# Column sums of the second norm in two groups, their last squares added on VectorE, and two chains of weight sums woven together

## The chip, the cores and the metric

The kernel runs on one core of one Trainium2 chip. The metric is the device time of one execution in microseconds; lower is better. Inputs and outputs are float32 and lie in device memory (HBM).

## The reference

One decoder layer on 1024 tokens with 1024 channels, and a final norm. Cut to what matters here:

```python
xn = rmsnorm(x, norm_mix_w)
proj = xn @ w_in                              # 1024 x 4352: queries, keys, values, gates
merged = sigmoid(g_da) * (diff_attention(...) @ w_br_da) + sigmoid(g_sw) * (window_attention(...) @ w_br_sw)
x = x + merged @ w_mix_out
xn = rmsnorm(x, norm_ffn_w)                   # x * rsqrt(mean(x*x) + eps) * w, per token
u = xn @ w_up                                 # 1024 x 5632
c = causal depthwise convolution of width 3 over u, + bias
gate, val = split(c)
x = x + (silu(gate) * val) @ w_down
return rmsnorm(x, norm_final_w)
```

## The kernel before

**Layout.** All activations are held transposed: 128 channels on the partitions, the 1024 tokens along the free dimension, cut into two halves of 512. Each float32 operand is split into a rounded high part (a cast on ScalarE, names that end in `h`) and a low part (the difference, on VectorE, names that end in `l`); one product of 128 x 128 weights with 512 tokens is then three matmuls: high by high, high by low, low by high.

**Products.** The large products (projections, mix, up projection, down projection) take a pair of weight chunks at once by a Strassen-Winograd scheme: seven products P1 to P7 of twelve matmuls each (4 chunks of the contraction by 3) instead of eight. Their operands are the blocks and some sums of them: `A11`, `A12`, `A22`, `S1` to `S4` of the weights, `B11`, `B21`, `B22`, `T1` to `T4` of the activations. Each product fills one PSUM bank (tiles `t`, 8 banks in rotation), so the eighth bank after it must be free again. `recombine` (L502 to L521 hold its callers and steps) empties them: one copy on ScalarE (`s`, L512) and seven steps on VectorE (L514 to L521), which give the two output chunks `us`.

**Stages.** `project` does the projections: five plain chunks, then nine pairs (`self.pairs`). `attention` follows, with some gate products between. `rest` merges the branches; `mix` does the mixing product and builds the operands of the up projection; `hidden` runs the up projection over 22 pairs `j` (a gate chunk and a value chunk each), with convolution and gating behind each pair; `down` does the down projection and the last norm.

**Order.** Each engine runs its instructions in one fixed order; a scheduler makes it from the order in the program, and the program bends it. `issue_after(i)` says that what is traced in its block stands behind `i` on that engine; it is an order, not a wait. In `mix` the work is laid out by a table `due`, whose entries are two letters: for instance `h40 l40` are the high and low part of T4's block 0. Each entry joins the end of one of two chains, `tails[0]` on VectorE and `tails[1]` on ScalarE.

**The second norm.** It needs, per token, the sum of squares over all channels. ScalarE squares each chunk of x; GpSimd adds the squares into `acc` (the tile `rstd`, one row of 512 for each half of the tokens, L945). The last four squares of the first half of the tokens (`self.sq`, in two tiles named `rv`) are not added to it. `col_sums` (L207) then sums over the partitions with matmuls of one column against a vector of ones: for each block of 128 tokens one matmul for each tile that is to be summed, so 4 x 5 for the first half and 4 x 1 for the second. `rstd_cols` makes the mean (`ms`, VectorE, L214) and its power -1/2 (GpSimd, L216); `spread` (L222) lays the result along the tokens, and ScalarE copies it into `rstd` (L1158). In the up projection the norm is applied late, to the products: L1235 multiplies `us` with `rstd`, ahead of the convolution (L1249, L1251, L1252).

In `hidden`, pair 0 runs P1, P5, P3, P7, P6, then the column sums, then P2 and P4. P4 needs T4, whose splits are the last entries of `due`.

**Weight sums.** The Strassen sums S1 to S4 of the projections' weights are made on GpSimd (L143 to L146, tiles `sf`) from two loaded chunks (`raw`, `rv`). For the mix weights (`md`) and the first two pairs of the up weights (`ud`, NPRE = 2) they are made by DMA in device memory, during the projections: copies issued by SyncE (L97, L109) and adding DMAs issued by GpSimd (L98, L110). `sums_of` (for md) is 32 such steps and `sums_up` (for ud) 16; a step that adds goes onto what a copy step before it wrote. The loop over the nine pairs takes a few steps of the chained generators in each pair: six in pairs 0 to 5, four in pairs 6 to 8; first all steps of md, then those of ud. SyncE's steps stand behind the pair's weight load, GpSimd's behind the pair's four sums.

For pair 1 of the up projection the weights come ready from `ud`: `part_pair` loads, casts and splits them in four parts, A11 and A12, S1 and S2, S3 and S4, A22 (L121, L126, L128). From pair 2 on `sum_pair` and `split_pair` do it (L138 to L146, L157, L159). The buffers of `raw` are three, so a load waits until the third part before it is split.

Of the kernel before, what the change touches and what calls it, by code (L numbers as in the profile page):

```python
# [3 lines left out]

# [1 line left out]

# [12 lines left out]
P = 128  # L19
# [4 lines left out]
H2 = 512  # L24
# [4 lines left out]
NPRE = 2  # L29
# [17 lines left out]
class Trunk:  # L47
# [27 lines left out]
    def ahead(self, n):  # L75
        while len(self.wq) < n and self.wsrc and (self.wsrc[0][1] != "pair" or self.uw):
            src, nk, *eng = self.wsrc.pop(0)
            if nk == "pair":
                first, skip = eng or (False, 0)
                if len(src) == 3:  # L80
                    w = {}
                    for part in range(4):
                        w.update(self.part_pair(src, part))
                    self.wq.append(w)
                else:
                    self.wq.append(self.split_pair(*self.sum_pair(src, first), skip))
            else:
                self.wq.append(self.load_w(src, nk, *eng))
        for i in range(min(2, len(self.wsrc)) if self.deep else 0):
            if len(self.wsrc[i]) == 2:  # L90
                self.wsrc[i] += None, None, self.load_raw(*self.wsrc[i])

    def sums_of(self, d, src, n):

        nc = self.nc
        row = lambda m, r: src[m].rearrange("p k c -> p (k c)")[:, r * n:(r + 1) * n]
        copy = lambda n, src: lambda m: nc.sync.dma_start(d[n][m], src(m))  # L97
        add = lambda n, o, r: lambda m: nc.gpsimd.dma_start(d[n][m], row(m + o, r), accum_op=ALU.add)  # L98
        for step in (copy("P5", lambda m: row(m + 4, 0)), copy("P7", lambda m: row(m + 4, 0)), add("P5", 4, 1), add("P7", 0, 0),
                     copy("P6", lambda m: d["P5"][m]), add("P6", 0, 0), copy("P3", lambda m: d["P6"][m]), add("P3", 0, 1)):  # L100
            for m in range(4):
                step(m)
                yield

    def sums_up(self):

# [201 lines left out]
    def project(self):  # L308
# [6 lines left out]
        with ExitStack() as ctx:  # L315
# [7 lines left out]
            acc = self.rstd  # L323
# [3 lines left out]
            ps = [[bank() for _ in range(2)] for _ in range(3)]  # L327
# [44 lines left out]
            with tc.tile_pool(name="xrp", bufs=6, reuse_waits="tile") as xrp:  # L372
# [69 lines left out]
                ssq = bank()  # L442
# [31 lines left out]
            for m in self.plain[3:]:  # L474
# [4 lines left out]
                if m == self.plain[3]:  # L479
                    with tc.issue_after(self.pow.ins), tc.high_priority(40):  # L480
                        wg, pg = self.next_w(), [bank() for _ in range(2)]
                    for hf in range(2):
                        self.mm3(pg[hf], wg, self.xact, hf)
            prods = (("P1", "A11", "B11"), ("P2", "A12", "B21"), ("P5", "S1", "T1"), ("P7", "S3", "T3"), ("P3", "S4", "B22"),
                     ("P6", "S2", "T2"), ("P4", "A22", "T4"))
            sums = chain(self.sums_of(self.md, self.w_mix, H2), self.sums_up())
            for j, ms in enumerate(self.pairs):
                w = self.next_w()
                for _ in range(6 if j < 6 else 4):
                    with tc.issue_after(self.sync), tc.issue_after(self.sum):  # L490
                        next(sums, None)
                pp = {}
# [400 lines left out]
    def mix(self, M, mr, mctx):  # L893
# [82 lines left out]
        def run_due(i, m):  # L976
            for op in due.pop((i, m), "").split():
                ops[op[:-1]](int(op[-1]))
# [81 lines left out]
                    sqs[:] = [self.tl(uw, [P, 2, H2], "rv", bufs=2) for _ in range(2)]  # L1060
        self.uw = uw
        run_due(13, 1)
        assert not due
        self.tails = tails
        return w0

    def chain(self, tails, n, f, *a):

        with self.tc.issue_after(tails[n]):
            i = f(*a)  # L1070
        tails[n] = i.ins
        return i
# [12 lines left out]
    def hidden(self, w0):  # L1085
        nc, tc = self.nc, self.tc
        with self.hctx as ctx:
# [7 lines left out]
            for j in range(NF):  # L1095
                w, ps = ready.pop(j) if j else (w0, {})
                if j == 0:
# [6 lines left out]
                        ps[name] = self.tl(psF, [P, H2], "t")  # L1104
                        self.product(ps[name], w[a], b)
                    ssq = self.tl(psF, [P, H2], "t")
                    self.col_sums(ssq, [self.rstd[:, :H2], *self.sq], 4, 0)
                    self.col_sums(ssq, [self.rstd[:, H2:]], 4, 4)
                    with tc.high_priority(400), tc.issue_after(self.tails[0]):
                        rs = self.rstd_cols(ssq, 8, D)  # L1110
                    self.tails[0] = self.ms
                if j == NF - 1:
                    for n in range(2):
                        self.wsrc[n] += None, None, self.load_raw(*self.wsrc[n])
# [377 lines left out]
```

## Time and profile before

| | us |
|---|---|
| median of 3 runs | 1324.23 (1322.56 to 1325.07) |
| profiled execution, its own time | 1323.9 |
| its span on the core | 1321.8 |
| busy in the span: TensorE matmuls / weight loads | 1307.1 / 1089.1 |
| busy: VectorE / ScalarE / GpSimd | 1067.7 / 639.5 / 497.5 |

The span is the time from the first to the last instruction. The engines are named PE (TensorE matmuls), PEld (its weight loads), DVE (VectorE), ACT (ScalarE), POOL (GpSimd) and SP (SyncE); a q behind a name is its sequencer, which issues DMAs. A row of the timeline has the start and the duration in us, the engine, the line, the operation, out<-in by the program's names, the shape and the count of instructions merged in it; in brackets the idle time ahead of it and what ended it. Matmuls are pipelined: a matmul of 512 columns is shown with a duration of 0.39 us, though the next one starts 0.23 us later, so the pace is read from start to start. A group row has the busy time in us and the mean duration of one instruction in ns. A row of the list of waits has who waited for whom, the total in us, how often, and the longest.

### The profile page before, as it was taken

The page shows a single profiled execution, that of the slowest core. Times are in us where ns is not written, and L with a number is a line of the kernel's source. Part 1 is how long each engine was busy: PE and PEld are TensorE (multiplying, and loading weights), DVE is VectorE, ACT ScalarE, POOL GpSimd, SP SyncE. Part 2 cuts the span into 40 slices and gives each one's busy share as a digit, 9 for nine tenths or more (in the row PEclk, how much of TensorE's full clock was granted, in tenths as well). Part 3 has the DMA queues.
Part 4 walks back from the last instruction along what each step waited for, and adds up shares of the span by engine and source line. Part 5 has one row for each costly group of instructions (what it writes and reads, how often), then busy time and mean ns, then how long its engine had stood idle before and what let it go on. Part 6 is the DMA issues. An engine that isn't in the chain of part 4 may idle for free.

```text
span 1321.8 us, 17377 instructions
## 1 busy us (share of the span) xinstructions
PE 1307.1 (99%) x6194; PEld 1089.1 (82%) x6194; DVE 1067.7 (81%) x1512; ACT 639.5 (48%) x1010; POOL 497.5 (38%) x399
## 2 busy tenths in 40 slices
PE   9999999999999999999999999999999999999997
PEld 7888888788888878888888888888888888888886
DVE  8845764488888977657889999999999999896865
ACT  8522331276666765334764344344344335554543
POOL 0456675001111015753335566766766632000002
PEclk9999999999999999999989999999999999999999
DMA  8357977976544335659665436554626228953534
GB/s 301 127 151 209 256 184 197 304 202 169 139 131 117 124 120 207 168 169 291 187 177 175 152 123 165 140 202 134 210 86 163 88 76 268 334 173 117 165 98 147
DMA packets 85447, 229.58 MB, mean 174 GB/s; under 512 B 9457, under 2 KB 17265, under 8 KB 85105
## 3 DMA queue, kind: packets, MB, share of 16 engines
q1 hardware_dynamic: 63264, 187.04, 42.7%
q0 software_dynamic: 9216, 24.12, 10.9%
q10 hardware_dynamic: 12880, 17.31, 3.7%
q8 instruction: 49, 0.80, 0.3%
q14 instruction: 38, 0.30, 0.1%
HBM read 173.39 MB, written 84.41 MB: 195 GB/s over the span
## 4 chain that ended last, share of the span: by engine, by line
PE 85%; POOL 4%; issue 3%; DVE 3%; DMA 3%; ACT 2%; SPq 0%; POOLq 0%; DVEq 0%; ACTq 0%
PE t L1082 34%; PE y L1305 9%; PE d L1305 7%; PE m L1046 6%; PE g L199 4%; PE g L200 4%; PE g L201 4%; PE sc L687 3%; POOL us L502 2%; PE t L703 1%; PE t L207 1%; DMA ud<-in_w_up 1%; PE sc L200 1%; PE sc L199 1%; PE sc L201 1%
## 5 line engine op out<-in xcount | busy, mean ns | idle before, releaser
L180 DVE TENSOR_TENSOR wl<-raw,wh 128x1024 fp32r<-128x1024 f32 (+2 forms) x91 | 109.2, 1201 | 48.5 <-ACT wh L178 40.5
L178 ACT CAST wh<-raw 128x1024 fp32r<-128x1024 f32 (+2 forms) x91 | 80.5, 886 | 99.7 <-PE y L1305 49.6
L1235 POOL TENSOR_TENSOR us<-us,rstd 128x1024 f32<-128x1024 f32 x42 | 93.4, 2272 | 51.0 <-DVE us L520 31.2
L216 POOL TENSOR_TENSOR rs<-ms,mhalf 128x8 f32<-128x8 f32 (+2 forms) x9 | 13.3, 1477 | 237.2 <-DVE ms L214 231.0
L143 POOL TENSOR_TENSOR sf<-rv 128x512 f32<-128x512 f32 x29 | 56.1, 1936 | 109.1 <-DMA rv<-in_w_up 53.9
L159 DVE TENSOR_TENSOR sl<-sf,sh 128x1024 fp32r<-128x1024 f32 x58 | 76.4, 1317 | 9.8 <-ACT sh L157 9.8
L157 ACT CAST sh<-sf 128x1024 fp32r<-128x1024 f32 x58 | 60.2, 1046 | 45.0 <-POOL us L1234 21.8
L1249 ACT ACTIVATE c<-us,vecs 128x1024 f32<-128x1024 f32 x44 | 54.7, 1247 | 52.9 <-POOL us L1235 49.8
L1082 PE MATMUL t<-x,wh 128*128 128x512 f32 x240 | 79.7, 389 | 0.0
L199 PE MATMUL g<-xh,wh 128*128 128x512 f32 x176 | 71.1, 404 | 2.5 <-ACT g L616 1.4
L1252 DVE SCALAR_TENSOR_TENSOR c<-us,vecs,c 128x1024 f32<-128x1024 f32 x44 | 73.3, 1698 | 0.0
L1082 PE MATMUL t<-x,sh 128*128 128x512 f32 x220 | 72.6, 398 | 0.0
L200 PE MATMUL g<-x,wh 128*128 128x512 f32 x176 | 70.5, 401 | 0.0
L201 PE MATMUL g<-xh,wl 128*128 128x512 f32 x176 | 70.4, 400 | 0.0
L1251 DVE SCALAR_TENSOR_TENSOR c<-us,vecs,c 128x1024 f32<-128x1024 f32 x44 | 65.1, 1512 | 1.7 <-ACT c L1249 1.7
L145 POOL TENSOR_TENSOR sf<-raw,rv 128x512 f32<-128x512 f32 x29 | 54.1, 1866 | 32.1 <-DVE sl L159 32.1
L1305 PE MATMUL y<-h,wh 128*128 128x512 f32 (+1 forms) x224 | 65.3, 375 | 0.0
L159 DVE TENSOR_TENSOR wl<-raw,wh 128x1024 fp32r<-128x1024 f32 x29 | 63.1, 2175 | 0.3
L691 DVE CUSTOM_DVE_ANT_0 L<-sc,bias 128x128 f32<-128x128 f32 (+7 forms) x64 | 47.7, 752 | 17.9 <-PE sc L687 14.7
L670 POOL MEMSET aT<- 128x128 f32 x32 | 6.2, 205 | 142.2 <-PE t L716 103.9
L692 ACT ACTIVATE L<-L,sm 128x128 f32<-128x128 f32 (+7 forms) x64 | 49.6, 778 | 20.6 <-DVE sm L691 17.9
L1046 PE MATMUL m<-x,wh 128*128 128x512 f32 x192 | 58.9, 389 | 0.0
(349 smaller groups left out, 4094.7 us busy)
## 6 DMA issues: line engine op xcount, KB each, us to landing
u<-qd SPq DMA_DIRECT2D x72, 256.0 KB, 6.4
raw<-in_w_in SPq DMA_DIRECT2D x22, 512.0 KB, 5.6
raw<-in_w_up SPq DMA_DIRECT2D x22, 512.0 KB, 5.0
hd<-c SPq DMA_DIRECT2D x22, 512.0 KB, 2.6
sdP<-in_w_down POOLq DMA_DIRECT2D x16, 704.0 KB, 8.3
rv<-in_w_up SPq DMA_DIRECT2D x20, 512.0 KB, 4.2
hc<-hd SPq DMA_DIRECT2D x33, 256.0 KB, 5.2
gr<-gd SPq DMA_DIRECT2D x16, 512.0 KB, 4.6
```

The lines of the kernel that those rows point to most:

```text
L159: low = nc.vector.tensor_tensor(lo, src, hi.bitcast(F32), ALU.subtract)
L178: self.hi = nc.scalar.copy(wh, raw)
L180: self.lo = (eng or nc.vector).tensor_tensor(wl, raw, wh.bitcast(F32), ALU.subtract)
L199: nc.tensor.matmul(ps, wh[:, kc + o, :], ah, start=first and n == 0, stop=False)
L200: nc.tensor.matmul(ps, wh[:, kc + o, :], al, start=False, stop=False)
L201: nc.tensor.matmul(ps, wl[:, kc + o, :], ah, start=False, stop=last and n == len(kcs) - 1)
L1046: nc.tensor.matmul(ps, v[:, m % 2 * 4 + k, :], x, start=start and k == j == 0, stop=k == 3 and j == 2, skip_group_check=True)
L1082: nc.tensor.matmul(ps, (ah, ah, al)[p][:, k, :], (bh, bl, bh)[p], start=first and n == p == 0, stop=last and p == 2 and n == len(ks) - 1, ...
L1235: i = (nc.vector if m % NF == 0 else nc.gpsimd).tensor_tensor(us[:, 2:], us[:, 2:], self.rstd, ALU.mult)
L1251: nc.vector.scalar_tensor_tensor(c, us[:, 1:T + 1], cw[1], c, ALU.mult, ALU.add)
L1252: nc.vector.scalar_tensor_tensor(c, us[:, 0:T], cw[0], c, ALU.mult, ALU.add)
L1305: nc.tensor.matmul(ps, v[:, k - k0, :], x, start=start and k == i == 0, stop=k == HK - 1 and i == 2, skip_group_check=True)
```

## The change

The last four squares of the first half are added into `acc` by VectorE, at the end of `mix`, behind the splits of T4. The column sums then read `acc` alone, 4 + 4 matmuls instead of 20 + 4, and stand in two groups: those of the second half at the old place, those of the first half behind P2 and P4. In `ahead`, parts 1 to 3 of pair 1's weights stand behind `ms` on VectorE and part 0 no longer does (before, all four did, since `self.tails[0]` was set to `ms`). In the projections the steps of the two chains are woven: in turn four of md and two of ud, six in each of the first eight pairs and none in the ninth.

```diff
@@ ahead
                     for part in range(4):
-                        w.update(self.part_pair(src, part))
+                        with self.tc.issue_after(self.ms) if part else nullcontext():
+                            w.update(self.part_pair(src, part))
@@ new
+    def weave(self, *gens):
+
+        for _ in range(8):
+            for g, n in zip(gens, (4, NPRE)):
+                for _ in range(n):
+                    next(g)
+                    yield
@@ project
-            sums = chain(self.sums_of(self.md, self.w_mix, H2), self.sums_up())
+            sums = self.weave(self.sums_of(self.md, self.w_mix, H2), self.sums_up())
             for j, ms in enumerate(self.pairs):
                 w = self.next_w()
-                for _ in range(6 if j < 6 else 4):
+                for _ in range(6):
                     with tc.issue_after(self.sync), tc.issue_after(self.sum):
                         next(sums, None)
@@ mix
         run_due(13, 1)
+        for sq in self.sq:
+            add(acc[:, :H2], sq)
@@ hidden
                     ssq = self.tl(psF, [P, H2], "t")
-                    self.col_sums(ssq, [self.rstd[:, :H2], *self.sq], 4, 0)
                     self.col_sums(ssq, [self.rstd[:, H2:]], 4, 4)
+                    for i in (1, 6):
+                        name, a, b = prods[i]
+                        ps[name] = self.tl(psF, [P, H2], "t")
+                        self.product(ps[name], w[a], b)
+                    self.col_sums(ssq, [self.rstd[:, :H2]], 4, 0)
                     with tc.high_priority(400), tc.issue_after(self.tails[0]):
                         rs = self.rstd_cols(ssq, 8, D)
-                    self.tails[0] = self.ms
```

Line numbers shift by 8 to 13 behind the new function: the changed kernel's L215 is `col_sums` (L207 before), L222 is `ms` (L214), L1080 the chained work of `mix` (L1070), L1092 the products (L1082), L510 the product of `us` with `rstd` (L502), L118 the adding DMA into ud (L110).

TensorE at the start of the up projection, before. `t_6546` is the bank of P6, `t_6559` that of the column sums, `t_6588` that of P2, `t_6601` that of P4; of the rows of the column sums those of one block of tokens and of the second half are shown:

```order
L1082 MATMUL t_6546<-z_1093_6231,sl_6197 128x512
L207 MATMUL t_6559<-ones,rstd 128x1
L207 MATMUL t_6559<-ones,rv_6334 128x1 x2
L207 MATMUL t_6559<-ones,rv_6333 128x1 x2
...
L207 MATMUL t_6559<-ones,rstd 128x1 x4
L1082 MATMUL t_6588<-x_1110_6399,sh_6152 128x512 x2
...
L1082 MATMUL t_6601<-T_3_6332,wl_6474 128x512
```

And in the changed kernel, with `t_6550` the bank of P6, `t_6563` that of the column sums, `t_6568` that of P2, `t_6581` that of P4 and `t_6666` that of P1 of pair 1:

```order
L1092 MATMUL t_6550<-z_1093_6231,sl_6197 128x512
L215 MATMUL t_6563<-ones,rstd 128x1 x4
L1092 MATMUL t_6568<-x_1110_6399,sh_6152 128x512 x2
...
L1092 MATMUL t_6581<-T_0_6329,wh_6472 128x512 x2
...
L1092 MATMUL t_6581<-T_3_6332,wl_6474 128x512
L215 MATMUL t_6563<-ones,rstd 128x1 x4
L1092 MATMUL t_6666<-B_0_5751,wh_6618 128x512 x2
```

The sixteen matmuls that read the squares are gone, and four of the eight left stand behind P4.

VectorE from the last split of T4, before. `u` and `us` are the recombination of pair 0, `ms` the mean, `wl_6632`, `sl_6638`, `sl_6644`, `wl_6650` the low parts of pair 1's weights, `sl_6668` and `wl_6664` the first ones of pair 2's:

```order
L1070 TENSOR_TENSOR T_3_6332<-xm_5769,T_3_6332 128x512
L515 TENSOR_TENSOR u_1132_6617<-t_6546,s_1131_6616 128x512
L214 TENSOR_SCALAR ms_6584<-t_6559 128x8
L516 TENSOR_TENSOR u_1133_6618<-u_1132_6617,t_6533 128x512
L128 TENSOR_TENSOR wl_6632<-raw_6628,wh_6630 128x1024
L128 TENSOR_TENSOR sl_6638<-raw_6634,sh_6636 128x1024
L514 TENSOR_TENSOR us_6614<-s_1131_6616,t_6588 128x512
...
L159 TENSOR_TENSOR sl_6668<-sf_6656,sh_6666 128x1024
L514 TENSOR_TENSOR us_6796<-s_1172_6798,t_6691 128x512
L159 TENSOR_TENSOR wl_6664<-raw_6652,wh_6662 128x1024
L1235 TENSOR_TENSOR us_6614<-us_6614,rstd 128x1024
```

And in the changed kernel (`wl_6620`, `sl_6626`, `sl_6632`, `wl_6638` for pair 1, `wl_6652` and `sl_6656` for pair 2):

```order
L1080 TENSOR_TENSOR rstd<-rstd,rv_6334 128x512 x2
L1080 TENSOR_TENSOR rstd<-rstd,rv_6333 128x512 x2
L136 TENSOR_TENSOR wl_6620<-raw_6616,wh_6618 128x1024
L523 TENSOR_TENSOR u_1132_6605<-t_6550,s_1131_6604 128x512
...
L529 TENSOR_TENSOR us_6603<-u_1133_6606,t_6581 128x512
L222 TENSOR_SCALAR ms_6598<-t_6563 128x8
L136 TENSOR_TENSOR sl_6626<-raw_6622,sh_6624 128x1024
...
L167 TENSOR_TENSOR wl_6652<-raw_6640,wh_6650 128x1024
L167 TENSOR_TENSOR sl_6656<-sf_6644,sh_6654 128x1024
L1248 TENSOR_TENSOR us_6602<-us_6602,rstd 128x1024
```

The four adds are new; all seven steps of pair 0's recombination (L522 to L529) now stand ahead of `ms`, and parts 1 to 3 of pair 1's weights behind it.

GpSimd from the sums of the last pair of the projections, before (`ud_92` and `ud_93` are the two pairs of the up weights, `us` the projections' outputs):

```order
L145 TENSOR_TENSOR sf_1670<-raw_1665,rv_1667 128x512
L146 TENSOR_TENSOR sf_1670<-raw_1665,sf_1669 128x512
L110 DMA ud_92<-in_w_up 128x512
L502 TENSOR_TENSOR us_1644<-us_1644,rstd 128x1024
L110 DMA ud_93<-in_w_up 128x512
L110 DMA ud_92<-in_w_up 128x512
L110 DMA ud_93<-in_w_up 128x512
L502 TENSOR_TENSOR us_1786<-us_1786,rstd 128x1024
```

And in the changed kernel, where `mdP_90` is the last of the mix sums:

```order
L153 TENSOR_TENSOR sf_1672<-raw_1667,rv_1669 128x512
L154 TENSOR_TENSOR sf_1672<-raw_1667,sf_1671 128x512
L98 DMA mdP_90<-in_w_mix 128x512
L510 TENSOR_TENSOR us_1646<-us_1646,rstd 128x1024
L98 DMA mdP_90<-in_w_mix 128x512 x3
L118 DMA ud_92<-in_w_up 128x512
L118 DMA ud_93<-in_w_up 128x512
L510 TENSOR_TENSOR us_1790<-us_1790,rstd 128x1024
```

The last adds into `ud` were four, of two kinds, in the last two pairs; they are now two, behind those of the mix sums. Further up, pairs 2, 3, 5 and 7 have four adds into `md` and two into `ud` each, and pairs 0, 1, 4 and 6 none; before, pairs 1, 2 and 3 had four adds, 6 had four, and 4, 5, 7 and 8 two each.

1 line of the change is left out of this document (removed).

## The prediction

> **What bounds the kernel now.** I read the page first, then the stages (the table of windows), then the rows of each engine in order of time around the places that the change touches, then the list of waits. Page, part 1, and two kinds of windows (time busy on PE, PEld, DVE, ACT, POOL, then granted clock, DMA share, GB/s):
>
> ```profile
> PE 1307.1 (99%) x6194; PEld 1089.1 (82%) x6194; DVE 1067.7 (81%) x1512; ACT 639.5 (48%) x1010; POOL 497.5 (38%) x399
> 682.45:685.10 2.65, 2.65 (x26) 2.61 (x24) 2.65 (x6) 2.65 (x5) 0.00 (x0) 1.00 0.09 29
> 685.10:690.22 5.12, 5.12 (x26) 5.12 (x25) 1.61 (x3) 2.13 (x3) 0.10 (x1) 0.50 0.45 135
> 690.22:695.35 5.13, 5.13 (x13) 4.07 (x14) 3.03 (x4) 0.00 (x0) 3.99 (x4) 0.50 0.67 224
> 704.00:1099.00 395.00, 395.00 (x1748) 327.15 (x1747) 385.50 (x337) 163.10 (x173) 244.72 (x173) 1.00 0.46 140
> ```
>
> TensorE is busy nearly always, so time can come only from work that it need not do, from work that it does slowly, or from its few stalls. The windows show slow work: from 685.10 to 695.35, 10.25 us, its clock was granted at 0.50. And in the hidden stage (704 to 1099) VectorE is busy 385.50 of 395.00 us: TensorE is the bound, but VectorE stands 2.4% behind it.
>
> TensorE's rows there, with the first column sum, the last eight passes, the first matmuls of P2 and P4 of pair 0, P1 of pair 1, the spread of rstd and P5 of pair 1; ahead of them the column sums of the first norm, at 39 us:
>
> ```profile
> 39.36 1.84 PE L207 MATMUL t<-ones,rstd 128*128 128x1 f32 x16
> 41.07 0.48 PE L199 MATMUL t<-xh,wh 128*128 128x512 f32 x1
> 682.54 0.28 PE L207 MATMUL t<-ones,rstd 128*128 128x1 f32 x2
> 688.58 1.84 PE L207 MATMUL t<-ones,rstd 128*128 128x1 f32 x8
> 690.29 1.20 PE L1082 MATMUL t<-x,sh 128*128 128x512 f32 x2
> 695.47 0.62 PE L1082 MATMUL t<-T,wh 128*128 128x512 f32 x2
> 698.22 0.61 PE L1082 MATMUL t<-B,wh 128*128 128x512 f32 x2
> 703.66 1.03 PE L222 MATMUL t<-ident,rs 128*128 128x128 f32 x8
> ```
>
> A column sum is two passes, so the 24 of them are 48 passes. At full clock sixteen passes took 41.07 - 39.36 = 1.71 us (0.107 each) and the clock did not fall. The 48 ran from 682.54 to 690.29, 7.75 us, and the clock fell 2.6 us into them. P2's twelve matmuls behind them took 5.18 us (690.29 to 695.47), P4's twelve 2.75 (695.47 to 698.22).
>
> **Column sums: TensorE's side.** Before, 682.54 to 695.47 is 12.93 us for 48 passes and P2. The change leaves 16 passes, eight and eight with P2 and P4 between, and drops 32. Neither group (0.86 us) is as long as the 1.71 us that kept the clock at 1.00, so I take full clock: 1.71 + 2.75 = 4.46 us. Saved: 8.47 us.
>
> Not all arrives, since the second group waits for four adds on VectorE, and the spread for the norm. VectorE, GpSimd, SyncE and ScalarE there:
>
> ```profile
> 683.62 2.48 DVE L1070 TENSOR_TENSOR T<-xm,T 128x512 fp32r<-128x512 f32 x4
> 690.47 0.17 DVE L214 TENSOR_SCALAR ms<-t 128x8 f32<-128x8 f32 x1 [3.76 <-PE t L207]
> 692.28 1.22 DVE L128 TENSOR_TENSOR sl<-raw,sh 128x1024 fp32r<-128x1024 f32 x1
> 695.67 0.69 DVE L514 TENSOR_TENSOR us<-s,t 128x512 f32<-128x512 f32 x1 [2.17 <-PE t L1082]
> 697.47 2.25 DVE L128 TENSOR_TENSOR sl<-raw,sh 128x1024 fp32r<-128x1024 f32 x1
> 701.44 2.31 DVE L159 TENSOR_TENSOR sl<-sf,sh 128x1024 fp32r<-128x1024 f32 x1
> 704.71 1.53 DVE L159 TENSOR_TENSOR wl<-raw,wh 128x1024 fp32r<-128x1024 f32 x1
> 706.17 3.45 DVE L1235 TENSOR_TENSOR us<-us,rstd 128x1024 f32<-128x1024 f32 x2
> 690.72 1.66 POOL L216 TENSOR_TENSOR rs<-ms,mhalf 128x8 f32<-128x8 f32 x1 [4.45 <-DVE ms L214]
> 697.34 1.30 POOL L144 TENSOR_TENSOR sf<-sf,raw 128x512 f32<-128x512 f32 x1 [2.64 <-DMA raw<-in_w_up]
> 693.52 0.33 SPq L138 DMA_DIRECT2D raw<-in_w_up  x1
> 703.63 1.05 ACT L157 CAST wh<-raw 128x1024 fp32r<-128x1024 f32 x1 [1.86 <-PE t L1082]
> ```
>
> T4's splits end at 686.10 in either kernel. An add of 512 columns is costed like one of them, 0.60: the four end at 688.5. TensorE reaches the second group at 682.54 + 0.86 + 2 x 2.75 = 688.9, so the adds are just hidden; if they were not, each 0.1 us late is 0.1 us on TensorE. Then VectorE, in its new order: the low part of pair 1's first weights (1.14 from start to next start), seven steps of the recombination (0.60 each) and only then ms: 688.5 + 1.1 + 4.2 = 693.8, ms by 694.0, the power by 695.7. TensorE has done P1 and P2 of pair 1 by 688.9 + 0.86 + 5.5 = 695.3 and waits 0.4 us for the spread. It starts that at 695.7 and no longer at 703.66: TensorE gains 8.0 us there.
>
> **Column sums: VectorE's side.** The change gives VectorE 2.4 us of adds and lets it drop its waits of 3.76 us (for the column sums) and 2.17 us (for P2). New is a wait further on: SyncE's load of pair 2's raw weights follows the first split of pair 1's sums, which begins at 692.28 before and at 694.0 now. So it goes out at about 695.2, not 693.52, and lands 3.8 us later as before (693.52 to 697.34), at 699.0; with ScalarE's cast of 1.05 us, the two splits of L159 (1.53 and 2.31) end at about 703.9, and the product with rstd (L1235) starts there and not at 706.17. VectorE gains 2.3 us where TensorE gains 8.0: it is 5.7 us further behind from there on. Moving parts 1 to 3 of pair 1's weights behind ms costs nothing by itself: their first reader, P5 of pair 1, stands behind the spread.
>
> What can TensorE bear? The bank that P6 of a pair needs is freed by L518; the matmul with a low part waits for L180:
>
> ```profile
> 1065.40 0.68 DVE L518 TENSOR_TENSOR u<-u,t 128x512 f32<-128x512 f32 x1
> 1069.04 0.61 PE L1082 MATMUL t<-z,sh 128*128 128x512 f32 x2
> 1103.89 0.96 DVE L180 TENSOR_TENSOR wl<-raw,wh 128x768 fp32r<-128x768 f32 x1 [1.50 <-ACT wh L178]
> 1127.49 0.95 DVE L180 TENSOR_TENSOR wl<-raw,wh 128x768 fp32r<-128x768 f32 x1
> 1129.34 0.39 PE L1305 MATMUL d<-x,wl 128*128 128x512 f32 x1
> ```
>
> Late in the hidden stage the bank is free 1069.04 - 1066.08 = 2.96 us ahead, at the start of the down projection the weights 1129.34 - 1128.44 = 0.90 us. TensorE keeps of its 8.0 us what VectorE gained plus this margin: 2.3 + 0.9 = 3.2 by the tighter place, 2.3 + 3.0 = 5.3 by the other. Between the two places VectorE idles 1.50 us in one wait, which a late VectorE can use, but that wait is for a cast that TensorE's own progress releases. I take 3.8, nearer to the tighter place since it comes last.
>
> [...]
>
> **The woven sums.** The number of copies (48) and adds is the same; only their order changes. TensorE's waits in this stage, and their cause:
>
> ```profile
> PE g L199 <- DVE u L518: 1.1, 1, 1.1
> PE t L1082 <- DVE wl L159: 0.6, 1, 0.6
> POOL ud L110 <- DMA ud<-ud: 12.2, 2, 7.7
> 227.02 0.82 POOL L110 DMA_DIRECT2D ud<-in_w_up  x1 [4.46 <-DMA ud<-ud]
> 227.57 2.69 POOL L502 TENSOR_TENSOR us<-us,rstd 128x1024 f32<-128x1024 f32 x1
> 230.29 1.15 ACT L533 ACTIVATE hi<-us,vecs 128x1024 fp32r<-128x1024 f32 x1 [12.60 <-POOL us L502]
> 87.27 2.72 POOL L98 DMA_DIRECT2D mdP<-in_w_mix  x3
> ```
>
> Before, the last adds into ud stand on GpSimd in the same pair as the copy that they add to and wait 12.2 us for it; the product us is queued behind, ScalarE's cast behind that, VectorE's recombination behind that, and the first gate product waits 1.1 us for a bank. Woven, each add follows its copy by a whole pair (19.0 us: 84 matmuls at 395.00/1748), and the last pair has none. In pair 1 the three adds ahead of us (2.72 us) go too, and with them the lateness behind the 0.6 us wait. I count both: 1.7 us. Bounds: 0, and those 1.7 us. SyncE's copies from md and ud likewise wait for adds a pair or more old, so raw loads behind them are not held.
>
> **Sum.** 1.7 + 3.8 = 5.5 us. The profiled execution took 1323.9 us (span 1321.8 and 2.1 around it), 0.3 below the median of the runs, so I set no difference between the two: 1318.4 us.
>
> **Rivals.** (a) TensorE keeps all 8.0: 1323.9 - 1.7 - 8.0 = 1314.2. For it: not one wait of TensorE in the hidden stage. Against: a lag of 5.7 against margins of 3.0 and 0.9.
> (b) VectorE is the bound throughout, no margin is left: 1323.9 - 1.7 - 2.3 = 1319.9. For it: 97.6% busy; against: the 2.96 us.
> (c) VectorE gains nothing, because the raw load or GpSimd's sums come over 2 us later than worked out (SyncE now issues two large copies of the down weights ahead of these loads): only the margin of 0.9 and the 1.7 are left, 1321.3, or 1322.2 without the margin.
> (d) Slower: GpSimd becomes the bound in the projections. Four pairs now issue six adds each where the fullest before issued four. These rows give its work in such a pair:
>
> ```profile
> L98 POOL DMA_DIRECT2D mdP<-in_w_mix x16 | 15.7, 1105 | 0.6 <-issue 0.6
> L502 POOL TENSOR_TENSOR us<-us,rstd 128x1024 f32<-128x1024 f32 x15 | 43.6, 2971 | 2.8 <-DVE us L520 2.8
> 84.32 1.29 POOL L145 TENSOR_TENSOR sf<-raw,rv 128x512 f32<-128x512 f32 x1 [1.16 <-DVE sl L159]
> ```
>
> Six issues of 1.105, two products of 2.971 and four sums of 1.29 make 17.7 us; it decides above the pair's 19.0. If the two issues more (2.2 us) came to lie on TensorE's path in all four pairs, that is 8.8 us, without the 1.7: 1323.9 - 3.8 + 8.8 = 1328.9. Against it: by this sum 1.3 us of each such pair are left, and the extra issues stand behind both products of their pair.
> That the clock still falls I hold unlikely, and it would change little, since VectorE then sets the end all the same.
>
> **How the numbers follow.** What this measurement can tell from no change is about 0.2%, 2.6 us. Chances: forecast 0.50, (a) 0.15, (b) 0.13, (c) 0.13, (d) 0.09. Forecast, (a) and (b) lie below 1321.6, and of (c) a small part: faster 0.80. The rest of (c) and a weak (d): same 0.11; slower 0.09. The forecast's own range is 3.2 to 5.3 us with 0 to 1.7 us: 1316.9 to 1320.7. The range to state reaches to (a) and past (c): 1313.9 to 1323.2.
>
> **What would show it.** Clock 1.00 all through 680 to 700, and P4 of pair 0 directly behind P2; the second eight passes at about 689 with a wait under 0.3 us; spread at about 694 (1.7 earlier than 695.7), some 0.4 us of waiting. VectorE's first product with rstd some 4 us earlier than 706.17. Then, late in the hidden stage and at the start of the down projection, TensorE waits for L518 and for low parts, 4 us in sum; if there are none, it is (a). In the projections no wait for ud on POOL and no gap at the first gate product. The prediction is wrong if waits for VectorE start already at pair 2, if POOL's sums are late in pairs 2 to 7, or if the attention stage, which I leave as it is, shifts by over 1 us.

## The result and the profile after

The change made the kernel slower, not faster: 1328.33 us (median of 7 runs, 1327.06 to 1330.39) against 1322.56 us for the kernel before in the same sessions, a ratio of 1.0044 with a 95% interval of 1.0027 to 1.0061. The profiled execution, the slowest of the seven, took 1330.39 us with a span of 1328.6 us. The forecast was 1318.4.

| from the starts of matmuls, us | before | after |
|---|---|---|
| first gate product (the projections are done) | 237.96 | 244.27 |
| first column sum | 682.54 | 689.03 |
| first matmul of the down projection (`y`) | 1098.96 | 1102.75 |
| first matmul of its second chain (`d`) | 1128.88 | 1134.93 |
| end of the span | 1321.8 | 1328.6 |

So the projections cost 6.3 us, and the place of the column sums and the 400 us behind it, 446.34 before and 445.90 after from the first column sum to `d`, gave back 0.4. That 0.4 is what remains of three parts: up to the spread 6.38 us were saved (14.74 in place of 21.12), then 3.68 lost in the hidden stage (398.98 from the spread to `y`, in place of 395.30) and 2.26 from `y` to `d` (32.18 in place of 29.92). What is left of the difference in span, some 0.7 us, lies behind `d`.

At the column sums, the page's line on TensorE and VectorE and the table of windows (time busy on PE, PEld, DVE, ACT, POOL, then granted clock, DMA share, GB/s), kernel after:

```profile
PE 1304.9 (98%) x6162; PEld 1081.4 (81%) x6162; DVE 1076.9 (81%) x1516; ACT 636.2 (48%) x1010; POOL 502.7 (38%) x399
689.03:692.00 2.97, 2.97 (x19) 2.60 (x18) 2.97 (x6) 2.35 (x4) 0.00 (x0) 1.00 0.21 65
692.00:696.38 4.38, 4.38 (x25) 3.53 (x23) 4.28 (x7) 1.72 (x2) 0.23 (x3) 1.00 0.53 143
696.38:703.77 7.39, 5.73 (x26) 4.40 (x26) 7.32 (x12) 1.11 (x2) 2.63 (x2) 1.00 0.96 332
```

The clock stays at 1.00 here, and TensorE is idle only for the 1.66 us ahead of the spread. Its rows and those of the other engines there, in order of time for each engine, kernel after:

```profile
689.03 0.95 PE L215 MATMUL t<-ones,rstd 128*128 128x1 f32 x8
695.46 1.05 PE L215 MATMUL t<-ones,rstd 128*128 128x1 f32 x8
696.38 0.70 PE L1092 MATMUL t<-B,wh 128*128 128x512 f32 x2
703.77 1.09 PE L230 MATMUL t<-ident,rs 128*128 128x128 f32 x8 [1.66 <-POOL rs L224]
692.56 2.85 DVE L1080 TENSOR_TENSOR rstd<-rstd,rv 128x512 f32<-128x512 f32 x4
700.90 0.16 DVE L222 TENSOR_SCALAR ms<-t 128x8 f32<-128x8 f32 x1
700.98 2.35 DVE L136 TENSOR_TENSOR sl<-raw,sh 128x1024 fp32r<-128x1024 f32 x2
708.89 1.35 DVE L167 TENSOR_TENSOR wl<-raw,wh 128x1024 fp32r<-128x1024 f32 x1 [4.36 <-ACT wh L165]
712.40 4.54 DVE L1248 TENSOR_TENSOR us<-us,rstd 128x1024 f32<-128x1024 f32 x2
716.86 3.51 DVE L1264 SCALAR_TENSOR_TENSOR c<-us,vecs,c 128x1024 f32<-128x1024 f32 x2
733.55 2.42 DVE L167 TENSOR_TENSOR wl<-raw,wh 128x1024 fp32r<-128x1024 f32 x1
696.95 1.17 SPq L97 DMA_DIRECT2D sdP<-in_w_down  x2
702.22 2.07 SPq L146 DMA_DIRECT2D raw<-in_w_up  x3
707.80 1.05 ACT L165 CAST wh<-raw 128x1024 fp32r<-128x1024 f32 x1 [5.67 <-DMA raw<-in_w_up]
707.86 1.30 POOL L152 TENSOR_TENSOR sf<-sf,raw 128x512 f32<-128x512 f32 x1 [2.79 <-DMA raw<-in_w_up]
711.34 2.27 POOL L154 TENSOR_TENSOR sf<-raw,sf 128x512 f32<-128x512 f32 x1
```

From the first column sum to the first matmul of pair 1, TensorE took 7.35 us (689.03 to 696.38) where it took 15.68 before (682.54 to 698.22): 8.33 saved. VectorE shows where they went. To compare times, 6.49 is taken off (689.03 - 682.54). SyncE issues the first raw load of pair 2 at 695.73 (before: 693.52), behind two copies for the down projection's sums; GpSimd can go on with that pair's sums at 701.37 (697.34), ScalarE casts at 701.31, and VectorE, after a wait of 4.36, reaches the first product with rstd at 705.91 (706.17). It has gained 0.26 us, and loses more than that behind it: the product takes 4.54 and the first two steps of the convolution 3.51 where before they took 3.45 and 2.48, and GpSimd's sums run at the same time. In the kernel before, GpSimd was idle there for 6.19 us. The split of pair 3's first weights, at 727.06, is 2.35 us later than before (two rows of the kernel before, GpSimd's and VectorE's):

```profile
713.59 0.10 POOL L1234 MEMSET us<- 128x2 f32 x1 [6.19 <-DVE c L1252]
724.71 3.09 DVE L159 TENSOR_TENSOR wl<-raw,wh 128x1024 fp32r<-128x1024 f32 x1
```

TensorE, still 6.4 us ahead at the spread (697.28 against 703.66), therefore waits. Its list of waits in the kernel after (who for whom, total, times, longest):

```profile
PE t L1092 <- ACT wh L165: 3.8, 1, 3.8
PE t L230 <- POOL rs L224: 1.7, 1, 1.7
PE t L1092 <- DVE wl L167: 1.6, 2, 1.1
PE t L1092 <- DVE u L523: 1.3, 3, 0.6
PE y L1318 <- DVE wl L188: 1.2, 1, 1.2
```

The first and third lie in the projections. The other three are new, and lie at the up and the down projection: the spread, a PSUM bank that VectorE empties late (L523), and a late low part at the start of the down projection (`y`). Behind the spread the list thus names 2.5 us, while the starts of the matmuls show 5.9 lost (3.68 and 2.26); the rest is in delays too small for it. The last wait has a link of its own, again from the kernel after: ahead of that low part VectorE waits for SyncE's load of `x`. SyncE issues it at 1120.61, behind a weight load that goes out at 1118.89, when a split on VectorE ends.

```profile
1129.16 0.69 DVE L1324 TENSOR_TENSOR x<-x,y 128x512 f32<-128x512 f32 x1 [1.25 <-DMA x<-x2d]
1131.83 0.50 PE L1318 MATMUL y<-x,wl 128*128 128x512 f32 x1 [1.19 <-DVE wl L188]
```

The largest wait is in the projections, and it is new. GpSimd, SyncE, ScalarE and TensorE there, kernel after:

```profile
173.84 2.81 POOL L98 DMA_DIRECT2D mdP<-in_w_mix  x3
182.46 0.81 POOL L118 DMA_DIRECT2D ud<-in_w_up  x1 [2.47 <-DVE u L526]
178.89 6.73 SPq L97 DMA_DIRECT2D mdP<-mdP  x3
189.53 2.42 SPq L117 DMA_DIRECT2D ud<-ud  x2
192.68 0.38 SPq L546 DMA_DIRECT2D qd<-hi  x1
189.22 1.15 ACT L541 ACTIVATE hi<-us,vecs 128x1024 fp32r<-128x1024 f32 x1 [10.54 <-POOL us L510]
200.00 1.04 ACT L544 CAST hi<-us 128x1024 fp32r<-128x1024 f32 x1 [8.64 <-DMA qd<-hi]
200.95 1.04 ACT L165 CAST wh<-raw 128x1024 fp32r<-128x1024 f32 x1
202.04 0.50 PE L1092 MATMUL t<-xh,wh 128*128 128x512 f32 x1 [3.84 <-ACT wh L165]
204.09 0.80 PE L1092 MATMUL t<-xh,wl 128*128 128x512 f32 x1 [1.12 <-DVE wl L167]
```

Pair 6's six copies read sums onto which pair 5's adds are still being made. GpSimd issues those adds late, behind its pair's sums (170 to 183 us), and SyncE stands at the copies until they have landed. SyncE's own list of waits says so, kernel after, 170 to 206 us:

```profile
SPq L97 <- DMA mdP<-in_w_mix: 13.2, 4, 6.2
SPq L117 <- DMA ud<-in_w_up: 5.2, 2, 3.8
```

Behind the copies on SyncE is the store of `hi`, whose data is ready at about 190.4. It goes out at 192.68 and frees its buffer at 200.0; ScalarE's next cast into such a buffer waits 8.64 us, the cast of the next weights stands behind it, and TensorE waits for those.

The stall costs more than its length. Behind it the granted clock falls to 0.50 for 6.8 us (kernel after; the columns are those of the windows above):

```profile
202.42:209.24 6.82, 5.70 (x14) 4.10 (x13) 6.68 (x9) 1.99 (x3) 3.25 (x3) 0.50 0.52 196
```

TensorE works 5.70 us of that at half speed, an estimated 2.9 us lost. With the 5.4 us of waits in the list (3.8 and 1.6), less the 1.7 that the kernel before waited in this stage (1.1 and 0.6), that is 6.6 us, near the 6.3 measured.

### The profile page after: what moved, and what is told of

It is laid out like the page before. It is cut to its first block, busy times and chain, and to the rows that moved or that the text cites. A ratio compares the mean times of both kernels' runs of the same rounds, so it can differ in the third digit from the quotient of the medians.

```text
span 1328.6 us, 17307 instructions
## 1 busy us (share of the span) xinstructions
PE 1304.9 (98%) x6162; PEld 1081.4 (81%) x6162; DVE 1076.9 (81%) x1516; ACT 636.2 (48%) x1010; POOL 502.7 (38%) x399
## 4 chain that ended last, share of the span: by engine, by line
PE 61%; DVE 12%; issue 7%; DMA 5%; POOL 5%; ACT 1%; SPq 0%; POOLq 0%; DVEq 0%; ACTq 0%
PE t L1092 16%; PE y L1318 8%; PE d L1318 7%; PE m L1054 6%; PE g L207 4%; PE g L208 4%; PE g L209 4%; DVE wl L167 3%; PE sc L695 3%; DMA rv<-in_w_up 2%; DVE c L1264 2%; DVE c L1265 2%; POOL sf L151 1%; PE t L711 1%; PE sc L208 1%
## 5 line engine op out<-in xcount | busy, mean ns | idle before, releaser
L188 DVE TENSOR_TENSOR wl<-raw,wh 128x1024 fp32r<-128x1024 f32 (+2 forms) x91 | 112.7, 1239 | 46.7 <-ACT wh L186 37.0
L151 POOL TENSOR_TENSOR sf<-rv 128x512 f32<-128x512 f32 x29 | 59.7, 2060 | 97.0 <-DMA rv<-in_w_up 50.0
L1092 PE MATMUL t<-x,wh 128*128 128x512 f32 x240 | 80.8, 393 | 0.0
L207 PE MATMUL g<-xh,wh 128*128 128x512 f32 x176 | 71.1, 404 | 1.4 <-ACT g L624 1.4
L1092 PE MATMUL t<-x,sh 128*128 128x512 f32 x220 | 70.8, 389 | 0.0
L167 DVE TENSOR_TENSOR wl<-raw,wh 128x1024 fp32r<-128x1024 f32 x29 | 66.5, 2293 | 4.5 <-ACT wh L165 4.4
L167 DVE TENSOR_TENSOR wl<-rv,wh 128x512 fp32r<-128x512 f32 x29 | 50.5, 1742 | 10.9 <-ACT wh L165 10.9
```

The source lines that it names most:

```text
L167: low = nc.vector.tensor_tensor(lo, src, hi.bitcast(F32), ALU.subtract)
L188: self.lo = (eng or nc.vector).tensor_tensor(wl, raw, wh.bitcast(F32), ALU.subtract)
L207: nc.tensor.matmul(ps, wh[:, kc + o, :], ah, start=first and n == 0, stop=False)
L1092: nc.tensor.matmul(ps, (ah, ah, al)[p][:, k, :], (bh, bl, bh)[p], start=first and n == p == 0, stop=last and p == 2 and n == len(ks) - 1, ...
```

## The experiments

All were timed beside the kernel before (1322.96, 1323.07 and 1323.86 us in the three sessions, 31 to 35 runs each). "Up" is the time from the first matmul of the up projection to `d`, 460.25 in the profile before and 459.78 after. One profile of a kernel has its own luck: the attention stage, whose code nobody touched, took between 352.8 and 357.2 us in them (the two longest, b2 and b3, have 3.4 us there with the clock at 0.50), so medians decide. They decide to a microsecond or two: the ratio on record is not quite that of the medians (c1: 0.9980, by the medians 0.9968), and its interval is some 2 us to either side.

| kernel | median | ratio to before, 95% | first gate product | up |
|---|---|---|---|---|
| a1 column sums alone | 1325.81 | 1.0028 [1.0012, 1.0044] | 236.99 | 462.92 |
| a2 weave alone | 1327.03 | 1.0043 [1.0028, 1.0058] | 242.54 | 458.60 |
| a3 steps in another order | 1325.82 | 1.0030 [1.0016, 1.0044] | 238.12 | 462.03 |
| a4 copies from the input | 1321.82 | 0.9995 [0.9982, 1.0007] | 237.59 | 459.89 |
| b1 adds on GpSimd (on a1) | 1324.43 | 1.0012 [0.9998, 1.0026] | 235.65 | 458.51 |
| b2 down's copies later (on a1) | 1323.27 | 1.0008 [0.9995, 1.0021] | 236.29 | 462.01 |
| b3 parts free (on a1) | 1319.76 | 0.9985 [0.9971, 1.0000] | 237.09 | 456.34 |
| b4 a pair without steps | 1323.46 | 1.0007 [0.9995, 1.0018] | 236.69 | 461.56 |
| c1 both repairs | 1319.67 | 0.9980 [0.9967, 0.9992] | 237.41 | 456.01 |
| c4 squares on TensorE (on b3) | 1323.46 | 1.0006 [0.9991, 1.0020] | 236.50 | 458.59 |
| c5 down's copies later (on c1) | 1322.27 | 1.0000 [0.9984, 1.0015] | 237.13 | 459.38 |
| c6 parts free, weave as changed | 1325.37 | 1.0026 [1.0013, 1.0040] | 243.04 | 455.91 |

**The two parts apart (a1, a2).** a1 takes back the weave, a2 takes back all but the weave.

```diff
a1
-            sums = self.weave(self.sums_of(self.md, self.w_mix, H2), self.sums_up())
+            sums = chain(self.sums_of(self.md, self.w_mix, H2), self.sums_up())
-                for _ in range(6):
+                for _ in range(6 if j < 6 else 4):
```

> The change without the weave: the weight sums of the projections in the order of before, everything of the column sums as changed. Theory W (the weave loses it: by the profiles the changed kernel reaches the first gate product 6.3 us later, and the column sums bring about 0.5): 1322.1 us, within 0.2% of before, first gate product at about 238 us as before, clock 1.00 through the column sums. Rival P (the column sums bring the 3.8 us of the prediction, and something else eats them in the whole change): 1318.8. Rival Q (the column sums themselves lose): above 1325.

> The kernel before with the woven weight sums alone, column sums as before. Theory W: 1328.8 us, a TensorE stall of some 4 to 6 us in the projections (near 198 us), first gate product at about 244 us. Rival P: the weave is harmless by itself (1320.9 to 1322.6), and only both parts together lose.

Both lose: 2.9 us (1325.81 - 1322.96) and 4.1 us. Theory W was half right: the weave does lose, with the stall in its place (3.2 us from start to start at 197.99, the gate product at 242.54), but the column sums lose as well, as rival Q had it; rival P is out. Together the two would be 6.9, and the whole change lost 5.8, a difference smaller than the intervals. In a1's profile the clock falls too, right behind TensorE's wait of 1.89 us for a low part at the start of the down projection:

```profile
1127.34:1130.75 3.41, 3.41 (x9) 2.64 (x10) 3.41 (x5) 0.03 (x1) 0.00 (x0) 0.50 0.79 240
```

So an estimated 1.7 us (half of 3.41) of a1's "up" are the clock's. That a2's "up" is 1.6 us shorter than before with the same code there goes with the clock, told of below: 0.50 for 6.82 us in place of 10.25, by estimate 1.7 us (half of the 3.43 between them).

**Where the weave loses (a3, a4, b4).** All three keep every copy and add, and the column sums as changed.

```diff
a3, sums_of (the steps of sums_up in the same order)
-        copy("P5"), copy("P7"), add("P5"), add("P7"), copy("P6"), add("P6"), copy("P3"), add("P3")
+        copy("P5"), add("P5"), copy("P7"), copy("P6"), add("P6"), add("P7"), copy("P3"), add("P3")
a4, the copies of pair 6
-        copy("P3", lambda m: d["P6"][m])
+        copy("P3", lambda m: row(m + 4, 0))
-        copy(3, lambda j: d[j][:, 1])
+        copy(3, lambda j: row(j + NF, 0))
b4, project
-                for _ in range(6):
+                for _ in range(6 if j != 6 else 0):
```

> The whole change, with the eight groups of six steps in another order, so that a copy from a sum comes two pairs behind the add that it waits for, not one; still six steps a pair, four pairs with six adds. Theory S (SyncE: the copies of pair 6 wait for the adds of pair 5 and hold the store of hi and the raw loads behind them, so that ScalarE's next cast has no buffer): the stall of 4 to 6 us goes, 1322.5 us, first gate product at about 238. Theory G (GpSimd: six adds in a pair make its sums and products late whatever SyncE does): the stall stays or moves to another of the four pairs, 1327 to 1329.

> The whole change, but the six copies of pair 6 read an input row in place of the sum, so they wait for no add (same bytes, same queues; the last of the four summed weights of each pair is then another sum). Theory S: the stall goes, 1322.5 us. Theory G: it stays, 1327 to 1329.

> The whole change, but pair 6 issues no step, so that the copies from the sums come two pairs behind the adds that they wait for (pair 7) and the last adds in pair 8; everything else in its order. Theory S (SyncE held by copies that wait for adds of the pair before): the stall near 198 us goes, first gate product at about 238 us, and the time is that of the column sums alone or of the copies from the input: 1322 to 1325.8. Theory G (six adds in a pair): still a stall of over 2 us in pair 5 to 8, above 1327.

All three bring the first gate product back to 236.7 to 238.1 us and the time down by 2.5 (a3), 6.5 (a4) and 4.9 us (b4) against the whole change, and in none of the three does the clock fall there. b4 keeps to what was expected. a3 does not: 1325.8 and not 1322.5, which is what the column sums alone cost (a1), a loss that its expectation left out. a4 is 4.0 us below a3, of which 2.1 show in "up"; why is open. a4 is the sharpest, since nothing moved: every engine has the same instructions in the same order, and only what six copies wait for is gone (`sums_of` also serves the down projection, so four copies of its sums changed their source too, in the up projection). Its SyncE and ScalarE rows:

```profile
179.50 1.28 SPq L117 DMA_DIRECT2D ud<-in_w_up  x2
190.40 0.33 SPq L546 DMA_DIRECT2D qd<-hi  x1
189.22 1.15 ACT L541 ACTIVATE hi<-us,vecs 128x1024 fp32r<-128x1024 f32 x1 [10.38 <-POOL us L510]
195.72 1.05 ACT L544 CAST hi<-us 128x1024 fp32r<-128x1024 f32 x1 [4.36 <-DMA qd<-hi]
```

GpSimd's product, and with it the cast of L541, ends the wait at 189.22 in both kernels, to the hundredth. So GpSimd is not what differs, and theory G falls. The store goes out at 190.40, when its data is ready, in place of 192.68, and frees the buffer 5.3 us later (to 195.72) in place of 7.3 (192.68 to 200.00): of the 4.28 us between the two casts 2.28 are SyncE's queue and 2.00 a slower store. That GpSimd's six adds cost something is visible too, since the same cast came at 186.84 in the kernel before; that is covered by other work.

**Where the column sums lose (b1, b2, b3).** All on a1.

```diff
b1, mix
-            add(acc[:, :H2], sq)
+            nc.gpsimd.tensor_tensor(acc[:, :H2], acc[:, :H2], sq, ALU.add)
b2, hidden
-                    for _ in range(2 if j else 0):
+                    for _ in range(2 if j > 1 else 0):
b3, ahead
-                        with self.tc.issue_after(self.ms) if part else nullcontext():
-                            w.update(self.part_pair(src, part))
+                        w.update(self.part_pair(src, part))
```

> The column sums alone (weight sums as before), and the four adds of the last squares on GpSimd, which is idle there for 8 us, in place of VectorE. Against the column sums alone (1325.8 us). Theory R (the raw load of pair 2 goes out 2.5 us later than before and lands 6.2 us later in place of 3.8, GpSimd's sums come 4.9 us late, and VectorE runs behind from there to the end): everything on VectorE stands 2.9 us earlier, so does that load, 1322.9 to 1323.4. Theory E (VectorE sets the end and only its added work counts): 2.9 us less as well, 1322.9. Theory D (the time is lost at the start of the down projection, whatever comes before): 1325.8.

> The column sums alone, and SyncE's copies for the down projection's sums begin one pair later, so that the two copies of 1.4 MB in sum no longer stand ahead of the raw load of pair 2; VectorE's work is the same. Theory R: the load lands some 3.8 us after its issue in place of 6.2, and the end comes 2.4 us sooner: 1323.4. Theory E and theory D: no change, 1325.8.

> The column sums alone, without the wait of pair 1's parts for ms: VectorE's first split of pair 1's sums stands ahead of most of the recombination again, so its buffer comes free and the raw load of pair 2 goes out some 3 us sooner; ms comes about 1 us later. VectorE's work is the same. Theory R: 2 to 3 us less, 1323 to 1324. Theory E and theory D: 1325.8; above that, where TensorE's wait for the spread grows by the 1 us and counts.

b3 leaves VectorE's work as it is and brings 6.0 us, so theory E, by which only the added work counts, is out. So is D, by which what comes before does not matter: b3 changes only that, and its wait at the start of the down projection is 0.5 us where a1's is 1.9. Much of the loss did lie there, though: from `y` to `d` a1 took 34.41 us and b3 31.52, 2.9 of the 6.6 us between their "up". b2 brings 2.5 us, within the noise of the two intervals, but its profile shows what it was made to test: the first of GpSimd's sums that waits for the raw load starts 3.74 us after the load's issue (696.72 to 700.46), in a1 6.21 (695.99 to 702.20). That profile is of the slowest of b2's runs (1326.44) and still has a wait of 2.4 us at `y`, with the clock at 0.50 for 3.4 us behind it. b1 brought 1.4 and not 2.9, and is a poor test: GpSimd's adds are in no chain and ran in the last stage of the mix, VectorE ended T4's splits at 689.76 us (in a1 it is at the adds behind them from 686.33 on), TensorE waited 1.3 and 1.6 us at 673 and 682, and the clock fell at 685.63 for 3.4 us. b3 is the largest effect of all, from one order. Its rows:

```profile
690.71 1.05 PE L215 MATMUL t<-ones,rstd 128*128 128x1 f32 x8
693.55 0.34 SPq L146 DMA_DIRECT2D raw<-in_w_up  x1
706.00 4.55 DVE L1248 TENSOR_TENSOR us<-us,rstd 128x1024 f32<-128x1024 f32 x2
710.48 2.68 DVE L1264 SCALAR_TENSOR_TENSOR c<-us,vecs,c 128x1024 f32<-128x1024 f32 x2
724.68 2.04 DVE L167 TENSOR_TENSOR wl<-raw,wh 128x1024 fp32r<-128x1024 f32 x1
```

Counted from the second group of column sums, the raw load goes out at 2.84 us (after: 6.76, 702.22 - 695.46), the first product starts at 15.29 (16.94), and the split of pair 3 at 33.97 (38.09). The 4.1 us that VectorE is ahead there are more than the 1.65 at the first product: GpSimd is through with its sums in time, and the convolution takes 2.68 in place of 3.51.

**Both repairs, and three checks (c1, c4, c5, c6).** c1 is the change with b3's and b4's edits. c6 has b3's alone, c5 adds b2's to c1. c4 is b3 without the four adds; TensorE sums the squares in the second group, 40 passes.

```diff
c4
-        for sq in self.sq:
-            add(acc[:, :H2], sq)
-                    self.col_sums(ssq, [self.rstd[:, :H2]], 4, 0)
+                    self.col_sums(ssq, [self.rstd[:, :H2], *self.sq], 4, 0)
```

> The whole change with both repairs: pair 6 issues no step, and pair 1's parts do not wait for ms. If theory S and theory R each name a whole cause and the two add: 1323.5 (the gap alone) less the 6.0 that the free parts brought to the column sums alone, some 1317.5 to 1319. If the weave takes something that the gap does not mend: 1320 or more, not better than the free parts with the order of before (1319.8).

> The column sums with free parts and the order of before in the projections, but the four adds on VectorE left out and the squares summed by TensorE again: 8 passes, then P2 and P4, then 40 passes. If VectorE sets the end from here on, the 2.9 us that it is spared count and TensorE's 3.4 us more do not, as long as the clock holds: 1317 to 1319. If TensorE does, or the clock falls to 0.50 in the 40 passes (some 3 to 8 us more on TensorE): 1321 to 1325.

> As the one with both repairs, and SyncE's copies for the down projection's sums begin one pair later. Theory R: the raw load of pair 2 is still one of two that stand behind those copies, so up to 2.4 us less than with both repairs. Rival: the raw load is early enough already, no change within 0.2%.

> The whole change with one repair alone: pair 1's parts do not wait for ms, the weave as it is. If the two causes add, the 6.0 us that the free parts brought to the column sums alone come here too: 1328.3 less 6.0 is 1322.3, with the stall near 198 us as in the changed kernel and the first gate product at about 244.

c1 beats both kernels: 4.2 us under the kernel before (1319.67 against 1323.86; 2.6 by the ratio, and the interval stays below 1) and 8.7 under the change. Of the change's three waits of TensorE in the up and down projections the one for a bank is gone, and two are left:

```profile
PE t L229 <- POOL rs L223: 1.6, 1, 1.6
PE y L1317 <- DVE wl L187: 1.1, 1, 1.1
```

It is no better than b3 by anything that these runs can tell, so for the woven order, once mended, no gain over the chained one is shown. c6, expected at 1322.3, has the stall of the weave (gate product at 243.04) and 3.0 us of b3's 6.0 (4.3 with each counted from the kernel before of its own session). The up projection is as short as in c1, so the repair does its work there, and the two medians apart (1328.33 and 1325.37) agree with that only in sign. c4 speaks for the adds on VectorE: without them 3.7 us more than b3 (2.9 counted from the kernel before of each session). 2.25 of them show in "up" (458.59 against 456.34), where the clock fell to 0.50 in the 40 passes and P1 of pair 1, right behind them, took 5.18 us (696.23 to 701.41), where P4 took 2.72 ahead of them (688.28 to 691.00); its profile also has a wait of 1.7 us at the start of the mix, which c6 has too (1.3) and the others have not, and which no edit explains. c5 was expected to gain or stay and came out 2.6 us above c1; its edit also turned two of GpSimd's sums of pair 2 around (L152 ahead of L151), VectorE then waits 4.83 us for the first of them in place of 3.77, and it does not test what it was meant to.

## Why the prediction was wrong, step by step

**The woven sums: wrong.** The failing step is "SyncE's copies from md and ud likewise wait for adds a pair or more old, so raw loads behind them are not held." The age was counted in pairs of the program. In the trace of the changed kernel SyncE is ahead of GpSimd there: it stands at the first of pair 6's copies from 168.93 to 175.24 us, and GpSimd issues the adds of the pair before from 170.92 to 182.46. What was held behind it was not only a raw load but a store whose buffer ScalarE needed. In place of 1.7 us less, the projections took 6.3 us more in the profile; a4, which takes those waits away, gives 6.5 us back, b4 4.9 and a3 2.5. And the sum had no term for the clock, which fell behind the stall and made up some 2.9 of the 6.3 us. The gain itself came in part: no add waits for ud any more, and the 1.1 us at the first gate product are gone, but in place of the 0.6 us wait for a low part there is one of 0.5.

**TensorE's side of the column sums: right.** 8.33 us saved where 8.47 were worked out, clock 1.00 through both groups, P4 directly behind P2, the second group not late. The wait at the spread is 1.66 us and not 0.4: the adds took 2.77 (692.56 to 695.33, where the next row starts) and not 2.4, and the power 2.57 and not 1.66.

**VectorE's side: wrong, by one sentence.** "Moving parts 1 to 3 of pair 1's weights behind ms costs nothing by itself." It looked for the first reader of those parts, P5 of pair 1, which is late enough, and not for what their splits release. The load of pair 2's raw weights had been counted, at 695.2; it came at 695.73. But the prediction took 3.8 us for its landing, though the copies for the down projection's sums now stand ahead of it (ScalarE's cast came 5.58 us after the issue, 702.22 to 707.80), and it kept the durations of before for the products and the convolution, though GpSimd's late sums now run beside them. So VectorE gained 0.26 us at the first product, not 2.3, and was 2.35 us behind at pair 3. Taking that one order away (b3) gives 3.3 us against the kernel before, near the 3.8 of the forecast; but the interval of that is 0 to 3.8 us, and b3 waits 1.6 us for the spread where 0.4 were counted, so the size agrees in part by luck.

**The margins: right in kind.** TensorE's waits came where they were expected, for a bank in the hidden stage (1.3 us) and for a low part at the start of the down projection (1.2 us). By the starts of the matmuls they cost more than the 4 us of the forecast, 5.9: 3.7 in the hidden stage and 2.3 from `y` to `d`. That the second runs over SyncE's load of `x` was not seen.

**The rivals.** (d) had the right sign and nearly the time (1328.9), by a cause that a4 rules out. (c) named what the column sums suffered from, a raw load over 2 us later than worked out, but priced it at nothing lost; alone they lose 2.9 us. (a) asked for 9.7 us less (1323.9 - 1314.2); the best kernel here, c1, has 4.2. (b) was right that VectorE sets the pace in the change as it stands (398.98 us from the spread to `y`), and wrong that it gains 2.3; with both repairs TensorE keeps its own pace there (c1: 395.38, the kernel before 395.30).

**Open.** Whether the two losses overlap at all (2.9 + 4.1 against 5.8), and why b3's repair is worth 6.0 us on a1 but 3.0 on the whole change. In the profiles the clock is part of the second: a1 has the 1.7 us at the start of the down projection, the change and c6 have no such fall there. Whether that holds for their other runs is not shown. a1's runs lie in two groups (four at 1322.4 to 1323.4, eight at 1325.5 to 1330.2); the profile is of the second.

## What to carry to other kernels

Before an instruction is moved behind another, follow not only who reads its result but which buffer it frees and which queue then goes on: here a split that nobody needed early held a load, the load held another engine's sums, and beside these the first engine took longer (4.54 and 3.51 us in place of 3.45 and 2.48). The age of a DMA's source counts in the order of the queues, not in iterations: here a queue that ran ahead met adds of the iteration before that had not been issued, waited 13.2 and 5.2 us for them, and what stood behind it waited too, a store that frees a buffer among it (ready at 190.4, issued at 192.68). The stall of TensorE cost more than its length: 3.8 us of waiting were followed by 6.8 at half the clock. And where two engines are as close as here, within 2.4% of each other, a saving on one is worth only what the other can follow: of the 6.4 us that TensorE was ahead at the spread 5.9 were lost behind it.

## What the runs showed of the hardware

**The clock fell while TensorE showed busy all the time, for 6.82 and for 10.25 us, and not at a fixed point.** In the same 48 passes it fell 2.6 us in and stayed at 0.50 for 10.25 us in the kernel before; in a2 it fell 4.1 us in. In the 40 passes of c4 it fell 3.5 us in. Windows of a2 (one microsecond each, granted clock in the third column from the end), and then of c4:

```profile
691.00:692.00 1.00, 1.00 (x7) 1.00 (x7) 0.19 (x1) 0.00 (x0) 0.00 (x0) 0.57 0.21 86
697.00:698.00 1.00, 1.00 (x4) 0.81 (x3) 0.00 (x0) 0.00 (x0) 0.73 (x3) 0.52 0.89 240
```

```profile
694.00:695.00 1.00, 1.00 (x9) 1.00 (x8) 0.96 (x3) 0.00 (x0) 0.00 (x0) 0.74 0.87 127
701.00:702.00 1.00, 1.00 (x5) 0.80 (x4) 0.00 (x0) 0.34 (x1) 1.00 (x2) 0.85 0.98 390
```

With 1.00 before and 0.50 behind, 0.57 puts a2's fall at 691.14 and 0.52 its rise at 697.96: 6.82 us. The same for c4 gives 694.48 and 701.30: 6.82 again. The fall in a1 has 3.41 us (1127.34 to 1130.75); 6.82 is twice that, and 10.25 three times. Whether it is the one-column passes that bring the clock down was not tried by itself, and what sets these lengths was not shown. With sixteen of them, in one group at the first norm (1.71 us) or in two of eight here (0.82 and 0.92 us, 689.03 to 689.85 and 695.46 to 696.38), it stayed at 1.00, but for b1, where TensorE had waited 1.5 us just ahead of the first eight. It fell behind waits alone as well: behind 1.89 us of waiting in a1 for 3.41 us, behind 3.84 in the change (and 1.12 more right after) for 6.82. Behind the 1.66 us at the spread it stayed at 1.00.

**VectorE and GpSimd took longer side by side.** The two products with rstd took 3.45 us before, where GpSimd's sums end in the middle of them (at 707.40), and 4.54 beside its sums; the convolution's two steps took 2.48 with GpSimd idle and 3.51 beside it. GpSimd took longer too: one of its sums took 1.30 us while VectorE waited (at 707.86) and another of the same shape 2.27 beside VectorE's work (at 711.34). Why they do was not shown.
